# Stationary-weight products by four blocks: thirty-two high-part matmuls into four PSUM tiles, then thirty-two low-part matmuls

## The chip, the cores and the metric

One Trainium2 chip, one of its NeuronCores. A program on this core runs on TensorE (PE in the profile; PEld is its weight load), VectorE (DVE), ScalarE (ACT), GpSimd (POOL) and SyncE (SP, which issues the transfers here). The metric is the device time of one execution in microseconds (us), lower is better.

## The reference

The reference runs two transformer blocks on 256 tokens of width 1024, in fp32. The second has two layers. What matters here are its wide products, which all have the form

```python
z = rmsnorm(h) @ W            # h: 256 x 1024, W: 1024 x n
a = square(relu(u2 @ w_up))                                  # first block, n = 4096
gate, up = split(h @ w_gu); y = (silu(gate) * up) @ w_down   # four times, n = 5632
q, k, v, conv parts = split(h @ w_mix_in)                    # twice, n = 3072
k, v = split(mem @ w_kv); q = h @ w_q                        # cross attention, twice
```

The kernel keeps fp32 accuracy: each operand is split into a high part and the rest, its low part, and a product is the sum of high x high, low x high and high x low.

## The kernel before

**Weights.** `Stream` brings the weights in one fixed order (`order_of_weights`). SP loads 1 MB raw pieces (L143). `prep` makes a *unit* of two raw chunks: ScalarE copies the high part `whi` (L154), VectorE subtracts it and leaves the low part `wlo` (L155). Each kind has six buffers (`W_BUFS`), so the next `whi` or `wlo` can be written only when TensorE has read the one six units earlier. `refill` calls `prep` once for each unit that was used.

**Products.** `linear` keeps the tokens stationary and streams the weights (L364 to L366). `linear_ws` does the reverse for `w_up`, the four gate-up products (`w_ffn*_gu`, called *gu* below), `w_mix_in`, `w_xq` and the key halves of `w_xkv`: the weights are stationary. A *group* is 512 outputs, four *blocks* of 128; one unit holds the weights of one block. A block has eight matmuls over 512 columns (`highs`, L403: high weights against the high and the low part of all 256 tokens) and eight over 256 columns (`lows`, L407: low weights against the high parts). All 16 accumulate in one PSUM tile of the block. There are four such tiles (`mm_tile`, tag `mm`, four buffers), taken in turn by both `linear` and `linear_ws`. The program has 70 groups in `linear_ws`; where `halves` is set, the first group of a product (seven in all) has a path of its own, L415 to L431.

**Evacuation.** When a block is done, `evac` lets ScalarE copy the right half of the tile at once (L446, waits for the block's lows), and pushes the rest as a chain of small steps on `side`: VectorE adds the left half (L447). This *add* is the last reader of the tile; a block that takes the same buffer four blocks later waits for it with its first high matmul. Then follow, for gu, a scaling by the row of norms (L917), Silu on ScalarE (L918), the product with the gate (L925), the high copy on ScalarE (L926) and the low part (L929). `side.pump` runs one such step at each call, two when over six chains are open.

**Order.** The order that the code is written in is not the order on the engines: the framework orders each engine's instructions when the program is built, and the order is then fixed. Each engine works its queue in that order.

The added line of the evacuation, and the two steps that it comes in:

```python
def added(dst, psum):
    ACT.activation(dst, psum[:, S:], AF.Copy)
    return lambda: V.tensor_tensor(dst, psum[:, :S], dst, op=ALU.add)
```

Of the kernel before, what the change touches and what calls it, by code (L numbers as in the profile page):

```python
# [17 lines left out]
P = 128  # L18
# [158 lines left out]
def order_of_weights():  # L177
    o = []

    def full(name, gs, nch):  # L180
        for g in gs:
            for c in range(0, nch, 8):
                o.append((name, g, c, min(8, nch - c)))

    full("w_in", range(8), 8)
    full("w_branch_pool", range(2), 4)
    full("w_branch_attn", range(2), 4)
    full("w_out", range(2), 8)
    full("w_xkv_0", (0,), 8)
    full("w_up", range(8), 8)  # L190
    full("w_down", range(2), 32)
    full("w_xkv_0", (1,), 8)
    for l in range(2):
        full(f"w_ffn1_gu_{l}", range(11), 8)
        full(f"w_ffn1_down_{l}", range(2), 22)
        full(f"w_mix_in_{l}", range(6), 8)
        full(f"w_xkv_{l}", (0, 1) if l == 1 else (2,), 8)
        for c in (4, 0):
            for g in range(2):
                o.append((f"w_mix_out_{l}", g, c, 4))  # L200
        full(f"w_xq_{l}", range(2), 8)
        full(f"w_xkv_{l}", (2, 3) if l == 1 else (3,), 8)
        for c in (0, 4):
            for g in range(2):
                o.append((f"w_xo_{l}", g, c, 4))
        full(f"w_ffn2_gu_{l}", range(11), 8)
        full(f"w_ffn2_down_{l}", range(2), 22)
    return o
# [3 lines left out]
def tile_two_blocks(ctx: ExitStack, tc: tile.TileContext, A: dict, out: bass.AP):  # L212
# [11 lines left out]
    side = Side()  # L224
    W = Stream(nc, wp, order_of_weights(), A)

    def mm_tile():
        return ps.tile([P, 512], F32, name="mm", tag="mm", bufs=4)
# [165 lines left out]
    def moving(lhs, c):  # L394
        for t in range(NT):
            side.want(lhs, (t, c))
        return lhs["m", c]

    def highs(psum, w, lhs, cs, st):


        for k, c in enumerate(cs):
            PE.matmul(psum, lhsT=w[:, k], rhs=moving(lhs, c), start=st and k == 0, stop=False)  # L403

    def lows(psum, w, lhs, cs, en):
        for k, c in enumerate(cs):
            PE.matmul(psum[:, :S], lhsT=w[:, k], rhs=lhs["m", c][:, 0], start=False, stop=en and k == len(cs) - 1)  # L407

    def linear_ws(name, gs, lhs, evac, halves=False):

        for g in gs:
            key = (name, g, 0, 8)
            if halves and g == gs[0]:  # L415
                pt = [mm_tile() for b in range(4)]
                for i in range(4):
                    half, bb = i // 2, i % 2
                    hi, lo = (w.rearrange("p a (c b q) -> p (a c) b q", b=2, q=P) for w in W.get(key, i)[:2])
                    cs = range(half * 4, half * 4 + 4)  # L420
                    for b in range(2):
                        highs(pt[2 * bb + b], hi[:, :, b], lhs, cs, half == 0)
                    side.pump()
                    for b in range(2):
                        lows(pt[2 * bb + b], lo[:, :, b], lhs, cs, half == 1)
                    W.refill()
                    side.pump()
                    if half == 1:
                        for b in range(2):
                            evac(g, 2 * bb + b, pt[2 * bb + b])  # L430
                continue  # L431
            for bb in (0, 2):
                pt = [mm_tile() for b in range(2)]
                w = [[u.rearrange("p a (c q) -> p (a c) q", q=P) for u in W.get(key, bb + b)[:2]] for b in range(2)]
                for b in range(2):
                    highs(pt[b], w[b][0], lhs, range(8), True)
                    side.pump()
                for b in range(2):
                    lows(pt[b], w[b][1], lhs, range(8), True)
                    W.refill()  # L440
                    side.pump()
                    evac(g, bb + b, pt[b])

    def added(dst, psum):

# [203 lines left out]
    def mem_keys(l, gs, lhs, pool, K):  # L649

        if not K:
            row = pool.tile([P, S], F32, name="row_mem")
            K["row"] = side.push(broadcast(row, rstd_mem))
            K["r"] = row
            K["kts"] = []
        for g in gs:
            K[g] = pool.tile([P, 2, 4, S], F32R, name=f"K{g}")

        def evac(g, b, psum):
            d = held("key")[:, :S]  # L660
            add = added(d, psum)

            def high():
                add()
                V.tensor_tensor(d, d, K["r"], op=ALU.mult)
                ACT.activation(K[g][:, 0, b], d, AF.Copy)

            def low():
                V.tensor_tensor(K[g][:, 1, b], d, K[g][:, 0, b].bitcast(F32), op=ALU.subtract)
            K["kts"].append(toks.add(side.push(high, low, deps=(K["row"],))))  # L670

        linear_ws(f"w_xkv_{l}", gs, lhs, evac)
# [175 lines left out]
    with tc.tile_pool(name="h1", bufs=1) as hp:  # L848
        lhs_a = {}

        def evac_up(g, b, psum):
            X = operand(lhs_a, g, hp, f"h{g}")
            a = held("up")[:, :S]
            add = added(a, psum)

            def high():
                add()
                V.scalar_tensor_tensor(a, a, 0.0, a, op0=ALU.max, op1=ALU.mult)
                ACT.activation(X[:, b, 0], a, AF.Copy)

            def low():
                V.tensor_tensor(X[:, b, 1], a, X[:, b, 0].bitcast(F32), op=ALU.subtract)
                give(lhs_a, X, 4 * g + b, 1, b)
            side.gives(toks.add(side.push(high, low)), lhs_a, [(t, 4 * g + b) for t in range(NT)])

        linear_ws("w_up", range(8), lhs_u2, evac_up, halves=True)
        rstd_f = {}
        lhs_f, evac_dn = post_norm("norm_mlp_post", [hp.tile([P, 512], F32, name=f"y{t}") for t in range(NT)],
                                      rstd_f, "ffn1_0", hp, rstd_u2)
        linear("w_down", range(2), 32, lhs_a, evac_dn, hold=True)  # L870
# [18 lines left out]
    def swiglu(l, which, lhs, rstds, gname):  # L889
        with tc.tile_pool(name=f"h{which}_{l}", bufs=1) as hp:  # L890
# [12 lines left out]
            def evac(g, b, psum):  # L903
# [27 lines left out]
                side.gives(pairs.add(side.push(high, low, deps=(gu["c"],))), lhs_h, [(t, 2 * g + j) for t in range(NT)])  # L931

            linear_ws(f"w_ffn{which}_gu_{l}", range(11), lhs, evac, halves=True)
            rn = {}
            nlhs, ev, _ = norm_residual(gname, rn, half_r)
# [321 lines left out]
    lhs, rstds = lhs_f, rstd_f  # L1257
    for l in range(2):
        last = l == 1
        lhs, rstds = swiglu(l, 1, lhs, rstds, f"mix_{l}")  # L1260
# [5 lines left out]
        with tc.tile_pool(name=f"v{l}", bufs=1) as vp:  # L1266
            with tc.tile_pool(name=f"mix{l}", bufs=1) as mp:
                lhs, rstds = mixer(l, lhs, rstds, mp, lhs_mem, K, Vp, vp)
            with tc.tile_pool(name=f"cr{l}", bufs=1) as mp:
                lhs, rstds = cross(l, lhs, rstds, mp, lhs_mem, K, Vp)  # L1270
        kt_ctx.close()
        lhs, rstds = swiglu(l, 2, lhs, rstds, None if last else "ffn1_1")
# [109 lines left out]
```

## Time and profile before

| | |
|---|---|
| median of 3 runs | 1518.08 us (1517.91 to 1520.4) |
| the profiled execution | 1518.06 us, its span 1516.2 us |
| TensorE busy | 1504.6 us, 99% of the span, 8026 matmuls |
| VectorE busy | 1061.2 us, 70% |
| ScalarE busy | 866.3 us, 57% |
| TensorE's granted clock | 0.999 of full speed over the span |

The span is the time between the first and the last instruction of the profiled execution; 1.9 us lie around it. Matmul times in the trace overlap, since the next one starts while the last drains: how long a matmul holds TensorE is read from start to start, not from its duration.

### The profile page before, as it was taken

What the parts mean: (1) busy time and instruction counts of PE and PEld (TensorE: products, weight loads), DVE (VectorE), ACT (ScalarE), POOL (GpSimd) and SP (SyncE); (2) the same over time, 40 slices, a digit from 0 to 9 for tenths busy, and PEclk for the clock granted to TensorE, in tenths of its full rate; (3) what the DMA queues carried; (4) which work ended last, traced back from release to release, by engine and by line L of the source; (5) the groups of instructions that cost most, each with busy time, mean ns of one, the idle gap of its engine ahead of it and who ended that gap; (6) DMA issues with size and microseconds to landing.
All of it is one profiled execution on the core that took longest, in us unless ns stands there. A gap on an engine that the chain in (4) does not pass through costs nothing.

```text
span 1516.2 us, 20937 instructions
## 1 busy us (share of the span) xinstructions
PE 1504.6 (99%) x8026; PEld 1284.0 (85%) x8026; DVE 1061.2 (70%) x1690; ACT 866.3 (57%) x1463; POOL 28.3 (2%) x43
## 2 busy tenths in 40 slices
PE   9999999999999999999999999999999999999998
PEld 7888888888888888888888888888888888888886
DVE  4758887448777557887677656776578887677753
ACT  6655666346665456656565545565466656566542
POOL 0000000000000000000000000000000000000000
PEclk9999999999999999999999999999999999999999
DMA  8565555545555464454455546554564454455552
GB/s 319 188 213 200 205 195 190 183 182 195 193 182 185 163 223 142 136 195 135 152 187 193 181 167 212 191 194 153 208 223 139 151 183 152 169 175 190 191 181 70
DMA packets 43734, 276.17 MB, mean 182 GB/s; under 512 B 5489, under 2 KB 6385, under 8 KB 12145
## 3 DMA queue, kind: packets, MB, share of 16 engines
q1 hardware_dynamic: 42912, 273.78, 52.9%
q8 instruction: 63, 1.03, 0.3%
q10 hardware_dynamic: 720, 1.05, 0.2%
q14 instruction: 39, 0.31, 0.1%
HBM read 273.76 MB, written 1.05 MB: 181 GB/s over the span
## 4 chain that ended last, share of the span: by engine, by line
PE 93%; DVE 4%; issue 1%; ACT 1%; DMA 0%; POOL 0%; SPq 0%; POOLq 0%; ACTq 0%; DVEq 0%
PE mm L403 32%; PE mm L407 16%; PE mm L364 13%; PE mm L366 13%; PE mm L365 13%; DVE wlo L155 2%; PE tp L612 1%; PE tp L310 1%; PE sc L575 1%; DVE lx L327 1%; PE tp L597 1%; DVE tmpT L304 1%; DMA raw<-in_w_in 0%; PE sc L1178 0%; ACT whi L154 0%
## 5 line engine op out<-in xcount | busy, mean ns | idle before, releaser
L155 DVE TENSOR_TENSOR wlo<-raw,whi 128x1024 fp32r<-128x1024 f32 (+1 forms) x505 | 612.2, 1220 | 288.3 <-ACT whi L154 178.7
L154 ACT ACTIVATE whi<-raw 128x1024 fp32r<-128x1024 f32 (+1 forms) x505 | 532.2, 1057 | 387.1 <-PE mm L403 209.4
L403 PE MATMUL mm<-lx,whi 128*128 128x512 f32 x2240 | 545.7, 393 | 2.7 <-DVE lx L327 2.2
L403 PEld LDWEIGHTS mm<-lx,whi 128*128 128x128 f32 x2240 | 408.9, 188 | 83.7 <-DVE lx L327 3.3
L407 PEld LDWEIGHTS mm<-lx,wlo 128*128 128x128 f32 x2240 | 289.5, 191 | 12.1
L407 PE MATMUL mm<-lx,wlo 128*128 128x256 f32 x2240 | 297.7, 283 | 0.0
L364 PE MATMUL mm<-whi,h 128*128 128x512 f32 x480 | 187.4, 390 | 0.0
L365 PE MATMUL mm<-whi,h 128*128 128x512 f32 x480 | 187.1, 390 | 0.0
L366 PE MATMUL mm<-wlo,h 128*128 128x512 f32 x480 | 186.8, 389 | 0.0
L364 PE MATMUL mm<-whi,lx 128*128 128x512 f32 x288 | 114.2, 397 | 0.0
L366 PE MATMUL mm<-wlo,lx 128*128 128x512 f32 x288 | 112.6, 391 | 0.0
L365 PE MATMUL mm<-whi,lx 128*128 128x512 f32 x288 | 112.3, 390 | 0.0
L366 PEld LDWEIGHTS mm<-wlo,h 128*128 128x128 f32 x480 | 90.1, 188 | 18.8
L364 PEld LDWEIGHTS mm<-whi,h 128*128 128x128 f32 x480 | 90.1, 188 | 18.4
L365 PEld LDWEIGHTS mm<-whi,h 128*128 128x128 f32 x480 | 90.2, 188 | 18.3
L446 ACT ACTIVATE gu<-mm 128x256 f32<-128x256 f32 x176 | 65.1, 375 | 21.7 <-PE mm L407 21.7
L925 DVE TENSOR_TENSOR gu<-gu 128x256 f32<-128x256 f32 x88 | 37.4, 425 | 42.3 <-ACT gu L918 42.3
L447 DVE TENSOR_TENSOR gu<-mm,gu 128x256 f32<-128x256 f32 x176 | 66.0, 417 | 0.0
L366 PEld LDWEIGHTS mm<-wlo,lx 128*128 128x128 f32 x288 | 54.1, 188 | 11.5
L365 PEld LDWEIGHTS mm<-whi,lx 128*128 128x128 f32 x288 | 54.2, 188 | 10.2
L364 PEld LDWEIGHTS mm<-whi,lx 128*128 128x128 f32 x288 | 54.2, 188 | 10.2
L347 ACT ACTIVATE junk<-x 128x512 f32<-128x512 f32 x44 | 27.6, 626 | 58.8 <-DVE x L466 50.2
(219 smaller groups left out, 1249.8 us busy)
## 6 DMA issues: line engine op xcount, KB each, us to landing
raw<-in_w_ffn_gu SPq DMA_DIRECT2D x88, 1024.0 KB, 4.9
raw<-in_w_ffn_down SPq DMA_DIRECT2D x40, 1024.0 KB, 4.9
raw<-in_w_mix_in SPq DMA_DIRECT2D x24, 1024.0 KB, 4.9
raw<-in_w_xkv SPq DMA_DIRECT2D x16, 1024.0 KB, 4.9
raw<-in_w_up SPq DMA_DIRECT2D x16, 1024.0 KB, 4.8
raw<-in_w_down SPq DMA_DIRECT2D x16, 1024.0 KB, 4.7
raw<-in_w_in SPq DMA_DIRECT2D x14, 1024.0 KB, 5.4
raw<-in_w_mix_out SPq DMA_DIRECT2D x8, 1024.0 KB, 4.9
```

Of the source, the lines that this page charges most:

```text
L154: self.nc.scalar.activation(hi[:, :n], raw[:, j:j + n], AF.Copy)
L155: self.nc.vector.tensor_tensor(lo[:, :n], raw[:, j:j + n], hi[:, :n].bitcast(F32), op=ALU.subtract)
L304: V.tensor_tensor(tmp, psum3, g_cols.unsqueeze(2).to_broadcast([P, n, P]), op=ALU.mult)
L347: ACT.activation(junk()[:, :src.shape[-1]], src, AF.Square, scale=scale, accum_out=s)
L364: PE.matmul(psum, lhsT=xl, rhs=hi[:, j], start=st, stop=False)
L365: PE.matmul(psum, lhsT=xh, rhs=hi[:, j], start=False, stop=False)
L366: PE.matmul(psum, lhsT=xh, rhs=lo[:, j], start=False, stop=en)
L403: PE.matmul(psum, lhsT=w[:, k], rhs=moving(lhs, c), start=st and k == 0, stop=False)
L407: PE.matmul(psum[:, :S], lhsT=w[:, k], rhs=lhs["m", c][:, 0], start=False, stop=en and k == len(cs) - 1)
L446: ACT.activation(dst, psum[:, S:], AF.Copy)
L447: return lambda: V.tensor_tensor(dst, psum[:, :S], dst, op=ALU.add)
L925: V.tensor_tensor(su, su, sg, op=ALU.mult)
```

## The change

Where `linear_ws` ran a group as two pairs of blocks (sixteen highs, sixteen lows, twice), it now takes all four PSUM tiles at its start, runs the 32 highs, then the 32 lows. `side.pump` is called after each block's highs and after each block's lows, as before; `refill` and `evac` come behind each block's lows. The first groups with `halves` are not touched. 63 groups are.

```diff
-            for bb in (0, 2):
-                pt = [mm_tile() for b in range(2)]
-                w = [[u.rearrange("p a (c q) -> p (a c) q", q=P) for u in W.get(key, bb + b)[:2]] for b in range(2)]
-                for b in range(2):
-                    highs(pt[b], w[b][0], lhs, range(8), True)
-                    side.pump()
-                for b in range(2):
-                    lows(pt[b], w[b][1], lhs, range(8), True)
-                    W.refill()
-                    side.pump()
-                    evac(g, bb + b, pt[b])
+            pt = [mm_tile() for b in range(4)]
+            for b in range(4):
+                w = W.get(key, b)[0].rearrange("p a (c q) -> p (a c) q", q=P)
+                highs(pt[b], w, lhs, range(8), True)
+                side.pump()
+            for b in range(4):
+                w = W.get(key, b)[1].rearrange("p a (c q) -> p (a c) q", q=P)
+                lows(pt[b], w, lhs, range(8), True)
+                W.refill()
+                side.pump()
+                evac(g, b, pt[b])
```

The order of the built programs differs in three places that matter below.

**VectorE in a gu product.** Before, a pair of blocks (tiles `mm_4060` and `mm_4061`) stands like this; `gu_4094` holds the pair's gate and up parts, `h` the finished operand, and the `wlo` rows are the weight units made for later:

```order
L155 TENSOR_TENSOR wlo_4091<-raw_3945,whi_4090 128x1024
L929 TENSOR_TENSOR h6_3986<-gu_4040,h6_3986 128x256
L155 TENSOR_TENSOR wlo_4106<-raw_3945,whi_4105 128x1024
L447 TENSOR_TENSOR gu_4094<-mm_4060,gu_4094 128x256
L447 TENSOR_TENSOR gu_4094<-mm_4061,gu_4094 128x256
L917 TENSOR_TENSOR gu_4094<-gu_4094,row_3254 128x256
L925 TENSOR_TENSOR gu_4094<-gu_4094 128x256
```

Now a whole group of four blocks (tiles `mm_4057` to `mm_4060`), the last two rows of its fourteen left off:

```order
L155 TENSOR_TENSOR wlo_4109<-raw_3944,whi_4108 128x1024
L155 TENSOR_TENSOR wlo_4124<-raw_3944,whi_4123 128x1024
L447 TENSOR_TENSOR gu_4112<-mm_4057,gu_4112 128x256
L155 TENSOR_TENSOR wlo_4142<-raw_4018,whi_4141 128x1024
L917 TENSOR_TENSOR gu_4112<-gu_4112,row_3254 128x256
L447 TENSOR_TENSOR gu_4112<-mm_4058,gu_4112 128x256
L155 TENSOR_TENSOR wlo_4159<-raw_4018,whi_4158 128x1024
L925 TENSOR_TENSOR gu_4112<-gu_4112 128x256
L447 TENSOR_TENSOR gu_4148<-mm_4059,gu_4148 128x256
L447 TENSOR_TENSOR gu_4148<-mm_4060,gu_4148 128x256
L929 TENSOR_TENSOR h7_4113<-gu_4112,h7_4113 128x256
L917 TENSOR_TENSOR gu_4148<-gu_4148,row_3254 128x256
```

The four subtractions of a group, whose buffers come free with the group's four blocks of lows, stood two by two between pairs that lay a pair of highs apart; now they stand around the first two adds.

**TensorE in a gu product.** Before, the same pair and the start of the next:

```order
L403 MATMUL mm_4060<-lx_3140,whi_3927 128x512 x4
L403 MATMUL mm_4060<-lx_3166,whi_3927 128x512 x4
L403 MATMUL mm_4061<-lx_3140,whi_3941 128x512 x4
L403 MATMUL mm_4061<-lx_3166,whi_3941 128x512 x4
L407 MATMUL mm_4060<-lx_3140,wlo_3928 128x256 x4
L407 MATMUL mm_4060<-lx_3166,wlo_3928 128x256 x4
L407 MATMUL mm_4061<-lx_3140,wlo_3942 128x256 x4
L407 MATMUL mm_4061<-lx_3166,wlo_3942 128x256 x4
L403 MATMUL mm_4115<-lx_3140,whi_3981 128x512 x4
```

Now, from the second block of a group to the first of the next (the first block's highs and one of its lows stand just ahead):

```order
L403 MATMUL mm_4059<-lx_3168,whi_3999 128x512 x4
L403 MATMUL mm_4060<-lx_3142,whi_4014 128x512 x4
L403 MATMUL mm_4060<-lx_3168,whi_4014 128x512 x4
L407 MATMUL mm_4057<-lx_3142,wlo_3924 128x256 x3
L407 MATMUL mm_4057<-lx_3168,wlo_3924 128x256 x4
L407 MATMUL mm_4058<-lx_3142,wlo_3941 128x256 x4
L407 MATMUL mm_4058<-lx_3168,wlo_3941 128x256 x4
L407 MATMUL mm_4059<-lx_3142,wlo_4000 128x256 x4
L407 MATMUL mm_4059<-lx_3168,wlo_4000 128x256 x4
L407 MATMUL mm_4060<-lx_3142,wlo_4015 128x256 x4
L407 MATMUL mm_4060<-lx_3168,wlo_4015 128x256 x4
L403 MATMUL mm_4166<-lx_3142,whi_4032 128x512 x4
```

`mm_4166` takes the buffer of `mm_4057`: a buffer was taken again after a whole other pair had run, and now is taken right behind the group's lows, of which 31 stand in one run.

**VectorE in the mixer, where the k group of `w_mix_in` ends.** `cB` are tiles of the forget gate's bias, made from transposes (`tp`, L1024 on TensorE) that `side` puts among the lows; `kT` rows at L447 are the adds of the group's blocks (`mm_5166` is the first). Before:

```order
L155 TENSOR_TENSOR wlo_5201<-raw_5036,whi_5200 128x1024
L155 TENSOR_TENSOR wlo_5214<-raw_5036,whi_5213 128x1024
L1026 TENSOR_TENSOR cB_4932<-tp_5219,c_mask_182 128x2x128
L447 TENSOR_TENSOR kT_4925<-mm_5166,kT_4925 128x256
L447 TENSOR_TENSOR kT_4925<-mm_5167,kT_4925 128x256
L1028 TENSOR_TENSOR cB_4932<-tp_5219,c_mask_182 128x2x128
L1026 TENSOR_TENSOR cB_4932<-tp_5238,c_mask_182 128x2x128
```

Now:

```order
L155 TENSOR_TENSOR wlo_5227<-raw_5036,whi_5226 128x1024
L1028 TENSOR_TENSOR cB_4932<-tp_5210,c_mask_182 128x2x128
L1026 TENSOR_TENSOR cB_4932<-tp_5230,c_mask_182 128x2x128
L155 TENSOR_TENSOR wlo_5248<-raw_5036,whi_5247 128x1024
L1028 TENSOR_TENSOR cB_4932<-tp_5230,c_mask_182 128x2x128
L1026 TENSOR_TENSOR cB_4932<-tp_5253,c_mask_182 128x2x128
L155 TENSOR_TENSOR wlo_5271<-raw_5129,whi_5270 128x1024
L1028 TENSOR_TENSOR cB_4932<-tp_5253,c_mask_182 128x2x128
L1026 TENSOR_TENSOR cB_4932<-tp_5274,c_mask_182 128x2x128
L155 TENSOR_TENSOR wlo_5292<-raw_5129,whi_5291 128x1024
L1028 TENSOR_TENSOR cB_4932<-tp_5274,c_mask_182 128x2x128
L447 TENSOR_TENSOR kT_4925<-mm_5166,kT_4925 128x256
```

The first add stood behind two subtractions and one `cB` row, and now stands behind all four subtractions and the seven `cB` rows between them.

## Rows read from the trace of the kernel before

**Rows 1.** The page's head, and busy time by engine.
```profile
span 1516.2 us, 20937 instructions
PE 1504.6 (99%) x8026; PEld 1284.0 (85%) x8026; DVE 1061.2 (70%) x1690; ACT 866.3 (57%) x1463; POOL 28.3 (2%) x43
```

**Rows 2.** The chain that ended last, by engine, then its largest lines.
```profile
PE 93%; DVE 4%; issue 1%; ACT 1%; DMA 0%; POOL 0%; SPq 0%; POOLq 0%; ACTq 0%; DVEq 0%
PE mm L403 32%; PE mm L407 16%; PE mm L364 13%; PE mm L366 13%; PE mm L365 13%; DVE wlo L155 2%; PE tp L612 1%; PE tp L310 1%; PE sc L575 1%; DVE lx L327 1%; PE tp L597 1%; DVE tmpT L304 1%; DMA raw<-in_w_in 0%; PE sc L1178 0%; ACT whi L154 0%
```

**Rows 3.** TensorE's waits: total us, times, longest us.
```profile
PE mm L403 <- DVE lx L327: 2.2, 5, 1.6
PE mm L403 <- DVE key L447: 0.5, 2, 0.3
```

**Rows 4.** Timeline of PE in a gu product: start, us, operation, count.
```profile
449.98 3.82 PE L403 MATMUL mm<-lx,whi 128*128 128x512 f32 x16
453.63 2.08 PE L407 MATMUL mm<-lx,wlo 128*128 128x256 f32 x16
455.55 3.82 PE L403 MATMUL mm<-lx,whi 128*128 128x512 f32 x16
...
461.11 1.09 PE L403 MATMUL mm<-lx,whi 128*128 128x512 f32 x4
```

**Rows 5.** Timeline of DVE in the same pair.
```profile
454.79 1.23 DVE L155 TENSOR_TENSOR wlo<-raw,whi 128x1024 fp32r<-128x1024 f32 x1 [0.94 <-PE mm L407]
455.93 0.42 DVE L929 TENSOR_TENSOR h<-gu,h 128x256 fp32r<-128x256 f32 x1
456.26 1.22 DVE L155 TENSOR_TENSOR wlo<-raw,whi 128x1024 fp32r<-128x1024 f32 x1
457.40 0.75 DVE L447 TENSOR_TENSOR gu<-mm,gu 128x256 f32<-128x256 f32 x2
458.06 0.42 DVE L917 TENSOR_TENSOR gu<-gu,row 128x256 f32<-128x256 f32 x1
```

**Rows 6.** Timeline around 1211.7 us, where TensorE waited for an add.
```profile
1211.25 0.41 DVE L447 TENSOR_TENSOR key<-mm,key 128x256 f32<-128x256 f32 x1
...
1211.78 0.76 PEld L403 LDWEIGHTS mm<-lx,whi 128*128 128x128 f32 x4 [0.47 <-ACT whi L154]
1211.81 0.93 PE L403 MATMUL mm<-lx,whi 128*128 128x512 f32 x3 [0.29 <-DVE key L447]
```

**Rows 7.** Groups of instructions by line: x count, busy us, mean ns, idle before.
```profile
L155 DVE TENSOR_TENSOR wlo<-raw,whi 128x1024 fp32r<-128x1024 f32 (+1 forms) x505 | 612.2, 1220 | 288.3 <-ACT whi L154 178.7 <-PE mm L407 85.9 <-PE mm L365 10.3
...
L858 DVE SCALAR_TENSOR_TENSOR up<-up 128x256 f32<-128x256 f32 x32 | 12.0, 417 | 0.0
...
L580 DVE TENSOR_REDUCE nm<-S 128x4 f32<-128x512 f32 (+1 forms) x12 | 11.3, 946 | 0.0
L964 DVE SCALAR_TENSOR_TENSOR S<-sc,cq,cB 128x128 f32<-128x128 f32 (+1 forms) x32 | 11.1, 409 | 0.0
```

**Rows 8.** Timeline of the mixer's k group: DVE, then PE.
```profile
581.00 2.36 DVE L155 TENSOR_TENSOR wlo<-raw,whi 128x1024 fp32r<-128x1024 f32 x2 [0.87 <-ACT whi L154]
583.28 0.42 DVE L1026 TENSOR_TENSOR cB<-tp,c_mask 128x256 f32<-128x256 f32 x1
583.61 0.75 DVE L447 TENSOR_TENSOR kT<-mm,kT 128x256 f32<-128x256 f32 x2
...
586.25 0.60 PE L1024 MATMUL tp<-c_ident,cq 128*128 128x128 f32 x4
586.60 1.20 PE L407 MATMUL mm<-lx,wlo 128*128 128x256 f32 x8
587.64 0.60 PE L1024 MATMUL tp<-c_ident,cq 128*128 128x128 f32 x4
587.99 1.19 PE L407 MATMUL mm<-lx,wlo 128*128 128x256 f32 x8
589.02 0.86 PE L403 MATMUL mm<-lx,whi 128*128 128x512 f32 x3
```

**Rows 9.** Busy time by engine in a stretch, with granted clock before DMA share.
```profile
174.00:178.00 4.00, 2.43 (x15) 1.97 (x14) 4.00 (x9) 2.81 (x6) 0.00 (x0) 1.00 0.75 258
```

## Prediction

> **What bounds the kernel now.** The page's head says that TensorE is busy 1504.6 of 1516.2 us [rows 1], and the chain that ended last is TensorE's for 93% and VectorE's for 4% [rows 2]. The list of TensorE's waits says how little it stands: the lines of these products, L403, waited 2.2 us for `lx` and 0.5 us for a key's add [rows 3]. So a change that leaves the matmuls as they are can gain about 2.7 us, and lose whatever wait it brings. What a matmul holds is read from start to start: sixteen highs from 449.98 to 453.63 are 3.65 us, 0.228 each, and sixteen lows to 455.55 are 1.92 us, 0.12 each [rows 4]. A group takes 2 x (449.98 to 455.55) = 11.1 us.
>
> The reader should see two slacks. VectorE's rows of the same pair [rows 5] show both adds over at 457.40 + 0.75 = 458.15, and the matmul that takes the first of these buffers again starts at 461.11 [rows 4]: 3.0 us early. And VectorE is the engine on which this hangs: a low part takes 1.22 us and the next instruction starts 1.14 after it (456.26, 457.40), a small step holds it about 0.335 (454.79 + 1.14 to 456.26) and ends after 0.42. Four low parts and ten small steps for each gu group are 4 x 1.14 + 10 x 0.335 = 7.9 of 11.1 us. It has room over the group, but not at every place in it.
>
> **The change, part by part.** No instruction is added or removed. The matmuls keep shape and number, so 32 highs and 32 lows cost 11.1 us as before; a low behind a low or behind a high costs the same 0.12. What moves is when a PSUM tile is free. All four tiles belong to one group, so the next group's first high waits for the add of block 0, which can only begin when block 0's lows are done, at the end of the group. The order decides the rest: on VectorE the first add stands behind two low parts, and the four low parts stand within 31 lows instead of two and two.
>
> *gu, forty groups.* Let 0 be the start of the 31 lows. Block 0 ends its lows after 7 x 0.12 = 0.84; VectorE starts a low part 0.20 after the lows that free its buffer (454.79, against 453.63 + 8 x 0.12 = 454.59), so at 1.04. The second starts at 2.18, the add at 3.32, and the add ends at 3.32 + 0.415 = 3.74. The lows are through at 31 x 0.12 = 3.72. A late add is seen once in this trace [rows 6]: it ends at 1211.25 + 0.41 = 1211.66 and the matmul starts at 1211.81, 0.15 later, and the first three matmuls then take 0.93 us where three take 0.86 without a wait [rows 8], 0.07 more. So the high starts at 3.89 instead of 3.72, and a boundary costs 0.17 + 0.07 = 0.24 us. The next adds: add 1 stands behind a third low part and a scaling, and from the first add's start at 3.32 it ends at 3.32 + 0.335 + 1.14 + 0.335 + 0.415 = 5.55; its high, a block of highs later (3.89 + 1.82 + 0.07), is wanted at 5.78 and needs it 0.15 earlier, 5.63. That fits by 0.08. Add 2 is behind one low part and one product more, 7.36 against 7.45, and add 3 a small step later against a whole block. So only the first wait counts: 40 x 0.24 = **+9.5 us**.
>
> *w_up, seven groups.* The first add is placed as in gu, 0.24. In every second group the second add stands behind a third low part, the product at L858 (0.417 long [rows 7]), a fourth low part and another small step: it ends 4 x 1.14 + 3 x 0.335 + 0.42 = 5.98 after the first low part's start, at 7.02. TensorE runs the first highs and, there, eight lows before the second highs, wanting them at 3.89 + 0.07 + 1.82 + 0.96 = 6.74: 0.43 late with the 0.15, and 0.07 for the restart. Boundaries then cost 0.24 + 0.5 and, in the other groups, about 0.2; three pairs and a last one are **+3 us**.
>
> *Mixer, two layers, five groups each.* Behind the k group the lows stand among four sets of transposes. Before, a set took from 586.25 to 586.60, and the eight lows behind it 1.04 instead of 0.96 [rows 8]: 0.44 in all. Run: 31 x 0.12 + 4 x 0.44 = 5.5 us. VectorE's first low part starts at 0.44 + 0.84 + 0.20 = 1.5; then four low parts and seven `cB` rows stand ahead of the add: 1.5 + 4 x 1.14 + 7 x 0.335 + 0.42 = 8.8, where before two low parts and one `cB` row stood ahead (581.00 to 583.61 [rows 8]). The high starts at 8.95 instead of 5.5 and costs 0.07: 3.5 us, and I take 3.6, since the sets use two buffers that VectorE also frees late: **+7.2** for two layers. Behind the zc group the late one is the second add. It stands behind three low parts, a row maximum L580 (mean 0.95, at least 0.6), three small steps and four S rows L964 (0.41 long, about 0.3 each on) [rows 7]: 3.42 + 0.6 + 1.0 + 1.2 + 0.42 = 6.6 from a start at 1.04, so 7.7, against about 6.2 where TensorE, with scores and transposes between its blocks, wants it: 1.6, **+3.2**. Behind zb the first add has three low parts ahead of it and ends at 1.04 + 3.42 + 0.42 = 4.88 against 3.84; 0.15 and 0.07 make 1.4, less two sets of transposes (0.8) that stand first: 0.6, **+1.2**. Behind q, with its transposes of `cums`, and behind uT, with eight and more small matmuls among the lows, nothing is late.
>
> *Keys of the second layer.* Their first adds too have three low parts ahead, and the second add a fourth and two small steps: about 1.8 between the two groups and 1.4 to what follows, less the 0.5 us that stood there before [rows 3]: **+2.7**.
>
> *Keys of the first layer.* Here the change removes a wait, the longest in the kernel, 1.6 us for `lx` [rows 3]. The chain of `lx` now has a group's 7.3 us of highs to finish in. But the later `lx` of the same token tile then comes about 0.7 us late, and the adds of the key groups cost some tenths: **-0.4**.
>
> The queue of SP is not touched by this: a group uses the same raw pieces in the same 11 us; the high parts on ScalarE move into the highs, where it has 57% to do [rows 1]. I cost that at nothing; were ScalarE late by a high part (1.06 us) once in a product, it would be under 8 us in all, and the range holds that.
>
> Sum: 9.5 + 3.0 + 7.2 + 3.2 + 1.2 + 2.7 - 0.4 = 26.4 us. The profiled execution took 1518.06 us, 1.9 more than its span, and the median is 1518.08, so the forecast stands on either: **1544.5 us**.
>
> **A rule to weigh.** The 1.6 us that TensorE waited left no mark on its clock: from 174 to 178 us, with the wait in it, the granted clock is 1.00 [rows 9], the 2.4 GHz level. The Trainium skill, in "TensorE: Matmul & The Clock Gate", section "A second HAM failure mode: psum-queue depth-cycling", describes a kernel that cycles through PSUM banks, whose TensorE idles a little between groups of matmuls so often that its clock swings between its two levels. By the trace the clock adds nothing to the sum; by that rule it is rival 4.
>
> **The rivals.** 1. *The tile is free in time (no slower, or a little faster).* The gu add is late by 0.02 us against the end of the lows; a weight load comes 0.03 ahead of its matmul at a restart and 0.12 after the add [rows 6]. If VectorE reached the add about 0.28 us earlier (one low part of 0.86 instead of 1.14 would do, or an order that lets the add go first), all forty waits would vanish; were the mixer's hidden as well, what is left is the `lx` wait that goes: 1518 - 1.6 = 1516.5, or no change if the keys eat it. Against it: the order has the two low parts ahead of the add, and 505 low parts have a mean of 1220 ns [rows 7], with no sign of a faster one. 7 in 100, 3 of them faster by over 0.2%. That bound, 3 us, is about what a measurement of this kernel can tell from no change.
>
> 2. *Less is lost.* If a boundary's restart costs only 0.1 and the mixer's TensorE work, as it slips, gives VectorE half its lateness back, gu is 4, w_up 2, mixer and keys 7: 13 us, 1531. For it: waits in a chain overlap, and one late add makes the next fit. 20 in 100.
>
> 3. *More is lost.* If every mixer boundary is as late as zc's or k's (10 more) and VectorE's rest of a group reaches into the next group's w_up and key adds (5 more), the time is 1560. For it: VectorE has 70% to do in the mean [rows 1], and what it falls behind in the mixer it carries on. 15 in 100.
>
> 4. *The clock falls.* If each of some 57 waits set the next block of highs (1.82 us) to the lower level of 1.2 GHz, it would take 1.82 us more: 57 x 1.82 = 104, and 1648 us. Against it: rows 9. 2 in 100. That is the case the page's rule would make.
>
> **How the numbers follow.** The forecast itself (1536 to 1553) has 56 in 100, rival 2 twenty, rival 3 fifteen, rival 1 seven, the clock two. The range from 1529 to 1561 takes in the forecast and most of rivals 2 and 3, and leaves out the first and the last and the far ends, some 15 in 100. Slower by over 0.2% is everything but rival 1: 93 in 100; the same 4; faster 3.
>
> **What would show it.** The list of TensorE's waits should have a new first row, L403 for gu's L447, with forty waits of 0.1 to 0.2 us, then rows for `kT` and `zc` (longest about 3.5) and for the second layer's keys; the `lx` wait should shrink. VectorE's busy time should stay at 1061 us, the clock at 1.00, and the highs and lows at 0.228 and 0.12. Wrong would be: VectorE's first add starting ahead of a low part, waits on `whi` or `wlo` (then weights, not PSUM, are late), or gu boundaries with no gap.

## The result, and the profile after

The changed kernel takes 1544.22 us in the median of four executions (1544.1 to 1547.25) against 1518.2, a ratio of 1.0174 (95% interval 1.0162 to 1.0187): slower by 26.0 us. The forecast was 1544.5. The profiled execution is the longest of the four, 1547.25 us; why it is 3 us over the others is part of the answer below.

The head of its page, with busy time by engine, answers to [rows 1]:

```profile
span 1545.3 us, 21062 instructions
PE 1520.9 (98%) x8026; PEld 1290.5 (84%) x8026; DVE 1056.4 (68%) x1690; ACT 881.3 (57%) x1463; POOL 27.1 (2%) x43
```

The work is the same: 8026 matmuls, 1690 VectorE instructions. VectorE is no busier (1056 us, 1061 before). The span grew by 29.1 us, so TensorE stood or ran slower. TensorE's waits (total us, times, longest) answer to [rows 3]:

```profile
PE mm L403 <- DVE kT L447: 6.2, 2, 3.1
PE mm L502 <- DVE junk L499: 1.5, 1, 1.5
PE sc L575 <- DVE S L964: 1.3, 2, 0.7
PE mm L403 <- DVE lx L327: 1.2, 4, 0.7
PE mm L364 <- DVE key L447: 1.0, 1, 1.0
PE mm L403 <- DVE up L447: 0.9, 3, 0.3
PE tp L1012 <- DVE lf L1008: 0.9, 2, 0.5
PE mm L364 <- ACT whi L154: 0.7, 2, 0.5
PE mm L403 <- ACT whi L154: 0.7, 1, 0.7
PE tp L612 <- DVE PT L599: 0.5, 2, 0.3
```

The 1.6 us wait for `lx` is gone (0.7 is the longest left), and the adds at L447 have come in its place. The list has no row for gu, though forty boundaries were to wait there. In the rows below, the record of the last low still runs (422.15 + 3.87 = 426.02) when the next high starts at 425.93, so the profile sees TensorE busy through the gap; only starts show it. TensorE's timeline through two gu groups, beside [rows 4]:

```profile
414.59 2.11 PE L403 MATMUL mm<-lx,whi 128*128 128x512 f32 x8
...
422.15 3.87 PE L407 MATMUL mm<-lx,wlo 128*128 128x256 f32 x31
425.93 2.11 PE L403 MATMUL mm<-lx,whi 128*128 128x512 f32 x8
...
433.46 3.87 PE L407 MATMUL mm<-lx,wlo 128*128 128x256 f32 x31
437.25 0.97 PE L403 MATMUL mm<-lx,whi 128*128 128x512 f32 x3
```

From 414.59 to 425.93 is 11.34 us, to 437.25 another 11.32, where a group took 11.13. The VectorE rows of the same place, beside [rows 5], show the two low parts and then the add, over at 425.46 + 0.42 = 425.88, the high at 425.93:

```profile
423.18 2.36 DVE L155 TENSOR_TENSOR wlo<-raw,whi 128x1024 fp32r<-128x1024 f32 x2 [1.73 <-PE mm L407]
425.46 0.42 DVE L447 TENSOR_TENSOR gu<-mm,gu 128x256 f32<-128x256 f32 x1
```

Behind the k group of the mixer the wait is plain, in the timeline of VectorE and TensorE that answers to [rows 8]:

```profile
596.31 1.21 DVE L155 TENSOR_TENSOR wlo<-raw,whi 128x1024 fp32r<-128x1024 f32 x1
...
597.44 0.42 DVE L1028 TENSOR_TENSOR cB<-tp,c_mask 128x256 f32<-128x256 f32 x1
597.77 0.74 DVE L447 TENSOR_TENSOR kT<-mm,kT 128x256 f32<-128x256 f32 x2
598.24 1.69 PEld L403 LDWEIGHTS mm<-lx,whi 128*128 128x128 f32 x7 [3.29 <-DVE kT L447]
598.24 1.98 PE L403 MATMUL mm<-lx,whi 128*128 128x512 f32 x6 [3.09 <-DVE kT L447]
```

And here the prediction's sum has no term for what follows. The windows behind this wait (after the engines' busy times, the granted clock stands ahead of the DMA share):

```profile
594.00:598.00 4.00, 1.15 (x10) 0.95 (x9) 4.00 (x8) 1.33 (x4) 0.00 (x0) 1.00 0.73 254
...
600.00:602.00 2.00, 2.00 (x6) 1.59 (x5) 0.94 (x3) 0.89 (x1) 0.00 (x0) 0.50 0.86 365
602.00:604.00 2.00, 2.00 (x8) 1.59 (x8) 0.00 (x0) 0.33 (x2) 0.00 (x0) 0.79 0.00 0
604.00:608.00 4.00, 4.00 (x24) 2.94 (x22) 1.64 (x5) 1.96 (x2) 0.00 (x0) 1.00 0.00 0
```

Soon after TensorE comes back, the granted clock is 0.50, the 1.2 GHz level, in which six highs fill 2 us instead of nine, and then 1.00 again. In the second layer, behind an equal wait, it stays at the lower level longer (13 slow highs instead of 7):

```profile
1170.00:1176.00 6.00, 5.71 (x13) 4.46 (x14) 3.00 (x9) 1.06 (x1) 0.00 (x0) 0.50 0.55 191
```

The table sets each stretch of the program against the kernel before, in us. A stretch runs from the first high of its first group to the first high of what follows it, as the two traces give them (the last one to the last matmul). Small matmuls that moved across a border count where they ran, so neighbouring rows are read together. e1 to e4 are the first four experiments, below.

| stretch | before | after | e1 adds first | e2 gu only | e3 mixer only | e4 k in pairs |
|---|---|---|---|---|---|---|
| keys 0, first layer | 14.93 | -1.31 | +0.40 | 0.00 | 0.00 | -1.31 |
| w_up and w_down | 176.29 | +3.45 | -0.17 | 0.00 | 0.00 | +3.39 |
| keys 1, first layer | 12.95 | +0.24 | +2.01 | -0.01 | -0.01 | +0.24 |
| gu, four products | 760.89 | +7.82 | -1.46 | +7.12 | +0.07 | +7.36 |
| q and k, layer 1 | 27.27 | +4.12 | +0.19 | 0.00 | +4.08 | +0.72 |
| zc, layer 1 | 14.47 | +1.73 | +0.87 | 0.00 | +0.06 | -0.04 |
| uT and zb, layer 1 | 66.89 | +1.57 | +0.08 | 0.00 | +1.61 | +1.61 |
| q and k, layer 2 | 27.27 | +4.18 | +0.30 | 0.00 | +4.14 | +0.77 |
| zc, layer 2 | 14.46 | +2.86 | +0.87 | 0.00 | +0.06 | -0.04 |
| uT and zb, layer 2 | 31.49 | +2.41 | +0.10 | +0.01 | +2.43 | +2.41 |
| keys, layer 2 | 47.37 | +1.74 | -0.39 | 0.00 | -0.40 | +1.79 |

### The profile page after: what moved, and what is told of

Its sections match the earlier page's. It is cut to its first block, busy times and chain, and to the rows that moved or that the text cites. A ratio compares the mean times of both kernels' runs of the same rounds, so it can differ in the third digit from the quotient of the medians.

```text
span 1545.3 us, 21062 instructions
## 1 busy us (share of the span) xinstructions
PE 1520.9 (98%) x8026; PEld 1290.5 (84%) x8026; DVE 1056.4 (68%) x1690; ACT 881.3 (57%) x1463; POOL 27.1 (2%) x43
## 4 chain that ended last, share of the span: by engine, by line
PE 88%; DVE 7%; ACT 2%; issue 1%; DMA 1%; POOL 0%; SPq 0%; POOLq 0%; DVEq 0%; ACTq 0%
PE mm L403 32%; PE mm L407 14%; PE mm L364 13%; PE mm L366 13%; PE mm L365 13%; DVE wlo L155 3%; PE tp L612 1%; ACT whi L154 1%; PE tp L310 1%; DMA raw<-in_w_in 0%; DVE lx L327 0%; DVE tmpT L304 0%; PE tp L597 0%; DVE S L964 0%; ACT junk L347 0%
## 5 line engine op out<-in xcount | busy, mean ns | idle before, releaser
L154 ACT ACTIVATE whi<-raw 128x1024 fp32r<-128x1024 f32 (+1 forms) x505 | 531.6, 1056 | 292.9 <-PE mm L365 148.8
L407 PEld LDWEIGHTS mm<-lx,wlo 128*128 128x128 f32 x2240 | 285.3, 191 | 10.0 <-issue 0.7
L364 PE MATMUL mm<-whi,h 128*128 128x512 f32 x480 | 188.0, 392 | 0.0
L364 PE MATMUL mm<-whi,lx 128*128 128x512 f32 x288 | 113.9, 396 | 1.2 <-DVE key L447 1.0
L364 PEld LDWEIGHTS mm<-whi,h 128*128 128x128 f32 x480 | 90.1, 188 | 19.0
L447 DVE TENSOR_TENSOR gu<-mm,gu 128x256 f32<-128x256 f32 x176 | 69.5, 416 | 0.5 <-ACT gu L446 0.5
L364 PEld LDWEIGHTS mm<-whi,lx 128*128 128x128 f32 x288 | 54.2, 188 | 11.8 <-DVE key L447 1.3
```

Of the source, the lines that this page charges most:

```text
L154: self.nc.scalar.activation(hi[:, :n], raw[:, j:j + n], AF.Copy)
L364: PE.matmul(psum, lhsT=xl, rhs=hi[:, j], start=st, stop=False)
```

## The experiments

The theory: what is lost is the wait for VectorE's add, the last reader of a PSUM tile, since the low parts of the coming weights stand ahead of it in VectorE's queue. The rivals: the order of the matmuls itself costs (through PSUM, or weights that come late); or VectorE's load, not its order.

**e1, the adds first.** In the changed kernel:

```diff
     def added(dst, psum):
         ACT.activation(dst, psum[:, S:], AF.Copy)
-        return lambda: V.tensor_tensor(dst, psum[:, :S], dst, op=ALU.add)
+        V.tensor_tensor(dst, psum[:, :S], dst, op=ALU.add)
+        return lambda: None
...
                 lows(pt[b], w, lhs, range(8), True)
+                evac(g, b, pt[b])
                 W.refill()
                 side.pump()
-                evac(g, b, pt[b])
```

> Four blocks as in the changed kernel, but each add is written in the evacuation itself, and the evacuation ahead of the refill, so that on VectorE an add stands behind at most one low part of its group instead of two to four. If the late adds are the cause, the 40 gu boundaries lose nothing (0.18 to 0.21 us each now), the 3.1 us waits behind the two k groups go, the clock stays at 1.00 there, and the time is 1516 to 1520 us. If the four-block order itself costs (weights that come late, or TensorE going through four PSUM tiles), the gaps stay and the time is 1538 to 1545 us. If the mixer's lateness is VectorE's load and not its order, gu is free and the mixer still waits: about 1530 us.

Measured: 1522.28 us (1521.25 to 1523.03), ratio to the kernel before 1.0025 (1.0015 to 1.0036). TensorE still runs 32 highs and then 32 lows, and 22 of the 26 us are gone. In a gu group VectorE now has the first add behind one low part, and TensorE's rows show 11.11 us from group to group (401.73 to 412.84):

```profile
401.73 7.44 PE L403 MATMUL mm<-lx,whi 128*128 128x512 f32 x32
409.01 4.00 PE L407 MATMUL mm<-lx,wlo 128*128 128x256 f32 x32
412.84 3.36 PE L403 MATMUL mm<-lx,whi 128*128 128x512 f32 x14
```

The waits for `kT` are out of the list and the clock is 1.00 behind the k groups. The expectation of 1516 to 1520 missed by 2 us. The list of the profiled execution, the shortest of the eight, says where: adds that go first push back another VectorE step, the low part of `lx`, which cost 2.2 us before [rows 3]:

```profile
PE mm L403 <- DVE lx L327: 4.1, 4, 2.1
```

**e2, gu alone**, and **e3, the mixer alone**. The pairs of the kernel before stand beside the four blocks under one condition, here that of e2; in e3 it is `'mix_in' in name`:

```diff
+            if '_gu_' in name:
+                pt = [mm_tile() for b in range(4)]
...
+            else:
+                for bb in (0, 2):
+                    pt = [mm_tile() for b in range(2)]
```

> Four blocks in the gu products alone, pairs everywhere else. Late adds: 40 boundaries of 0.18 to 0.2 us and nothing else, +7.5 us on the kernel before, about 1525.7 us, clock 1.00 throughout. If the gaps depended on what the other products leave behind, it would be under 1521 us.

Measured: 1525.46 us (1524.9 to 1525.74), ratio 1.0045 (1.0029 to 1.0062), clock 0.999. The forty boundaries are worth 7.2 us, and in the table nothing else moves.

> Four blocks in w_mix_in alone, pairs everywhere else. Each theory expects the 3.1 us wait behind the k group, twice. If the clock falls because of that one wait, the granted clock is 0.5 for a few us behind it here too, with no gu gaps in the program, and the time is 15 to 17 us over the kernel before, 1533 to 1535 us. If the clock falls because of the many small gaps before it, it stays at 1.00 here and the time is 10 to 12 us over, 1528 to 1530 us.

Measured: 1532.84 us (1530.12 to 1533.47), ratio 1.0092 (1.0077 to 1.0107). The profiled execution is the shortest, and has the full wait and no fall. TensorE's rows and then the windows behind the first k group:

```profile
593.18 5.73 PE L403 MATMUL mm<-lx,whi 128*128 128x512 f32 x24 [3.09 <-DVE kT L460]
```
```profile
593.00:595.00 2.00, 1.82 (x8) 1.52 (x9) 2.00 (x7) 0.00 (x0) 0.00 (x0) 1.00 0.79 184
595.00:597.00 2.00, 2.00 (x11) 1.65 (x10) 0.89 (x3) 1.06 (x1) 0.00 (x0) 1.00 0.90 377
```

The 24 highs take 5.73 us, where the same stretch of the changed kernel took 7.39. The waits are the same; whether the clock falls behind one is not. The other three executions are 2.1 to 3.4 us longer than this one, about what one or two falls cost, though without their traces that is inferred. So neither expectation held as written. The small gaps are not what it takes: e7, below, has none in gu, and the clock fell behind one of its two k groups.

**e4, the k groups in pairs.** The condition is `if not ('mix_in' in name and g == 2)`.

> The changed kernel with the two k groups of w_mix_in back in pairs. If the first add behind four low parts and seven rows of the forget gate's bias is what waits, both 3.1 us waits go and with them the fall of the clock (about 1.9 us behind the first wait, 3.0 behind the second): 10 us less than the changed kernel, about 1534 us; if the zc group's adds then wait as the prediction counted (1.6 us a layer), about 1537 us. If the wait is due to VectorE's load in the mixer, it moves to the next boundary, and the time is over 1541 us.

Measured: 1535.22 us, ratio 1.0111 (1.0096 to 1.0126), 9.0 under the changed kernel. `kT` is out of the list of waits, nothing has come in its place behind k or zc, the clock is 1.00 behind both, and the four executions lie within 0.4 us (1535.14 to 1535.46), where the changed kernel's lie within 3.2. That fits a scatter that comes from these waits, but does not show it: e1, which has none of them, lies within 1.8 us, and of the first four executions of the kernel before one took 1520.4.

**e5 and e6, the add made later.** A step more ahead of the first add of each gu group, into a tile that nothing reads: of 256 columns in e5, and in e6 of 1792, with both inputs broadcast seven times:

```diff
                     def gate():
+                        if b == 0 and g > 0:
+                            V.tensor_tensor(late, sg, row, op=ALU.mult)
                         add()
```

> The changed kernel with one small VectorE step more (the gate by the row, into a tile that nothing reads) ahead of the first add of each of the 40 gu groups; in the built order the add then stands behind a third low part and this step, 1.14 + 0.335 = 1.475 us more of VectorE. If TensorE waits for that add, each boundary grows by 1.475 us, 59 us in all, about 1602 us, with forty waits of about 1.5 us for gu's add in the list. If the gap of 0.18 to 0.2 us is a fixed cost of coming back to the first PSUM tile, it is under 1550 us. If waits of this length already lower the clock, as the fourth rival has it, the granted clock shows 0.5 behind the boundaries and the time is 1640 to 1680 us.

Measured: 1605.93 us (1604.45 to 1607.41), ratio 1.0576 (1.056 to 1.0593), 3.9 over what was expected of a wait for the add. TensorE's rows: 12.84 us from group to group, 1.5 more than in the changed kernel for 1.475 us more of VectorE.

```profile
406.07 7.54 PE L403 MATMUL mm<-lx,whi 128*128 128x512 f32 x32 [1.48 <-DVE gu L447]
...
418.91 7.52 PE L403 MATMUL mm<-lx,whi 128*128 128x512 f32 x32 [1.47 <-DVE gu L447]
```

By as much as VectorE's add is later, TensorE stands. The list has 36 such waits ahead of a high, and four of 1.4 to 1.5 us where a product ends. No fall of the clock follows any of them; over nine groups the window has

```profile
390.00:496.00 106.00, 92.73 (x528) 80.89 (x528) 71.22 (x126) 57.15 (x99) 0.00 (x0) 1.00 0.49 161
```

> As the run with one more small step, but that step is 128 x 1792, about 2.0 us, so that the add is late by 1.14 + 2.0 = 3.15 us at each of the 40 boundaries, as long as the wait behind the k group. Without any fall of the clock: 40 x 3.15 = 126 us more than the changed kernel, about 1669 us. If each wait of this length makes the clock fall, 1.7 to 2.9 us more at each, 1735 to 1785 us, with 0.5 behind every boundary. If it falls behind some waits and not behind others, as between the two executions of the mixer-only kernel, the time lies between and the profile shows both kinds.

Measured: 1742.19 us (1735.93 to 1747.14), ratio 1.1472 (1.1448 to 1.1497). The waits are 3.07 us, as meant, and groups with and without a fall stand side by side:

```profile
441.12 9.16 PE L403 MATMUL mm<-lx,whi 128*128 128x512 f32 x32 [3.07 <-DVE gu L447]
450.12 3.99 PE L407 MATMUL mm<-lx,wlo 128*128 128x256 f32 x32
457.18 7.52 PE L403 MATMUL mm<-lx,whi 128*128 128x512 f32 x32 [3.07 <-DVE gu L447]
...
487.65 10.18 PE L403 MATMUL mm<-lx,whi 128*128 128x512 f32 x32 [3.07 <-DVE gu L447]
```
```profile
441.00:446.00 5.00, 4.88 (x14) 3.87 (x15) 3.63 (x9) 2.09 (x4) 0.00 (x0) 0.66 0.61 198
...
457.00:462.00 5.00, 4.82 (x21) 4.04 (x22) 3.93 (x10) 2.98 (x5) 0.00 (x0) 1.00 0.57 188
...
486.60:487.60 1.00, 0.00 (x0) 0.00 (x0) 1.00 (x3) 0.00 (x0) 0.00 (x0) 0.50 1.01 418
```

Counted over the trace, by highs that start 0.4 to 0.6 us apart: the clock fell behind 28 of the 36 gu waits, for 6 to 8 highs (1.3 to 1.6 us lost; here 9.16 - 7.52 = 1.64) or for 13 (10.18 - 7.52 = 2.66). It fell behind the four waits at the ends of the products too. The profile shows both kinds, the third case of the expectation, though with so many falls the time lies in the range of the second.

**e7, gu's tile to ScalarE.** VectorE's order is left as in the changed kernel, and ScalarE alone frees the tile:

```diff
+    def copied(dst, psum):
+        ACT.activation(dst, psum, AF.Copy)
+        return lambda: V.tensor_tensor(dst[:, :S], dst[:, :S], dst[:, S:], op=ALU.add)
...
-                    gu["s"] = hp.tile([P, 2, S], F32, name="gu", tag="gu", bufs=3)
+                    gu["s"] = hp.tile([P, 2, 2 * S], F32, name="gu", tag="gu", bufs=3)
...
-                    add = added(sg, psum)
+                    add = copied(gu["s"][:, 0], psum)
...
```

> The changed kernel with VectorE's order as it is, but in gu ScalarE copies the whole tile to SBUF (512 instead of 256 columns, about 0.25 us more each) and VectorE adds the two halves there, so that PSUM is free without VectorE. If the gap is the wait for VectorE's release, the 40 gaps go: 7.5 us less, about 1536.7 us. If VectorE's order starves something else (low parts or operands), they stay and the time is 1543 to 1546 us. If the longer copies make ScalarE late with the high parts, it is slower than the changed kernel.

Measured: 1536.53 us (1536.14 to 1537.61), ratio 1.0121 (1.0107 to 1.0135), 7.7 under the changed kernel. VectorE's add still stands behind two low parts and ends at 424.89 + 0.42 = 425.31; TensorE has gone on at 425.30 without it, because ScalarE had the tile out at 422.63 + 0.58 = 423.21:

```profile
422.62 2.36 DVE L155 TENSOR_TENSOR wlo<-raw,whi 128x1024 fp32r<-128x1024 f32 x2 [1.85 <-PE mm L407]
422.63 0.58 ACT L445 ACTIVATE gu<-mm 128x512 f32<-128x512 f32 x1
...
424.89 0.42 DVE L446 TENSOR_TENSOR gu<-gu 128x256 f32<-128x256 f32 x1
...
425.30 6.08 PE L403 MATMUL mm<-lx,whi 128*128 128x512 f32 x26
```

That rules out the matmul order, PSUM itself and starved weights as the cause of the gu gaps. One detail of TensorE's order differs: the changed kernel runs one low of a gu group's first block among the highs, while e1, e5, e6 and e7 run all 32 lows together. The waits of e5 and e6 stand without that low, so it is not the cause either.

**e8, the parts that pay.** Four blocks in gu, with the adds first as in e1, and in the first layer's first key group; pairs elsewhere. `now` writes the copy and the add at once.

```diff
+            if '_gu_' in name or (name == 'w_xkv_0' and gs[0] == 0):
...
+                    if '_gu_' in name:
+                        evac(g, b, pt[b])
                     W.refill()
                     side.pump()
+                    if '_gu_' not in name:
+                        evac(g, b, pt[b])
...
-                    add = added(sg, psum)
+                    add = now(sg, psum)
...
```

> Four blocks only where the runs show a gain: the gu products, with each add written in the evacuation and ahead of the refill (0.19 us less a product than before), and the first key group of the first layer (1.3 us less there, 0.9 given back in the group behind it). Pairs everywhere else. About 1.2 us faster than the kernel before, 1517.0 us. If the adds that go first make the operand of the next product late, as in the run with the adds first, no gain or up to 2 us slower.

Measured: 1517.36 us (1516.77 to 1517.86, eleven executions) against 1518.31 (1517.83 to 1518.79), ratio 0.9994 (0.9985 to 1.0002). The medians lie 0.95 us apart, as forecast to 0.3 us, but the interval reaches over 1, so it is not shown to be faster. In its trace the key group gives 1.31 and w_up takes 0.89 back, as in the changed kernel, and the gu products give 0.8 together.

## Why the prediction was right, point by point

**The cause holds; that the sum came so close is in part luck.** The forecast sum was +26.4 us, the median came out at +26.0, but with an estimated 1.4 us of slow clock in it (below) that the forecast did not count, and with terms that missed both ways. The main step, that the first add ends just behind the run of lows because two low parts stand ahead of it, is shown from three sides: moving the add (e1), freeing the tile without it (e7), and delaying it (e5).

**The terms were less exact than the sum.** *gu*: predicted 0.24 a boundary and 9.5 in all, measured 7.2 (e2): 0.17 to 0.21 at most boundaries and 0.05 at the first of each product. The term that was mis-sized is the start behind the add: the high came 0.05 us behind the add's end (425.88, 425.93), not 0.15 as read from [rows 6], so the gap between lows and highs was 0.07 and not 0.17. The first high then held TensorE 0.10 longer than usual (0.33, not 0.23), near the 0.07 of the sum. *w_up*: 3.0 predicted. Seven boundaries gave 0.05 to 0.67 each, 2.55 together, alternating as the order said. *Behind k*: 3.6 predicted a layer, 3.1 of wait measured, which is 3.3 lost from the start of the last low to that of the high (3.45 us, where 0.12 is usual); with 0.4 to 0.5 where the transposes of `cums` wait for `lf`, which the prediction had put at nothing, q and k lose 4.1 together. *Behind zc*: the wait for zc's second add, 1.6, is not there (e4: -0.04, with nothing slowing the highs). VectorE's lateness shows one stretch on, where the scores wait 0.7 us for S and a transpose 0.3 for PT, 1.2 in all. The prediction had the lateness of VectorE right and the instruction that feels it wrong. *zb*: 0.6 predicted (by its own terms, 4.88 - 3.84 + 0.15 + 0.07 - 0.8, it is 0.5), 0.4 measured in the first layer and 1.2 in the second. But 0.8 of that 1.2 are eight transposes (L310) that ran among the matmuls of the next stretch before. First the rows of the kernel before, then those of the changed one:

```profile
1199.61 1.03 PE L310 MATMUL tp<-c_ident,att 128*128 128x128 f32 x8
1200.40 2.16 PE L407 MATMUL mm<-lx,wlo 128*128 128x256 f32 x16
```
```profile
1220.32 1.04 PE L310 MATMUL tp<-c_ident,att 128*128 128x128 f32 x8
1221.52 2.14 PE L403 MATMUL mm<-lx,whi 128*128 128x512 f32 x8 [0.17 <-DVE zb L447]
```

So zb is 0.4 late there too. *Keys*: second layer 2.7 predicted; the table has 1.7, and with the 0.8 that moved out of this stretch 2.5 are lost. In the first layer -0.4 was predicted; the first key group gave 1.3, w_up's first group took 0.9 back and the second key group 0.2, so -0.2. Over the mixer alone the errors cancel: 5.8 a layer predicted, in e3's shortest execution 5.75 and 6.6, with the 0.8 of the transposes in the second.

**The signs.** VectorE's first add did stand behind its low parts and the `lx` wait shrank. Three signs that the prediction named came out otherwise: the list has no row for gu and none for `zc`, and the clock did not stay at 1.00. Of its signs of being wrong one shows in part: TensorE waits 0.7 us for a high part, `whi`, once in the second layer's keys, and twice ahead of L364 (0.7 in all), where the kernel before has no such row. ScalarE's lateness, which was costed at nothing, is under 1.5 us in all.

**What the sum lacked was the clock.** The two falls behind the k groups cost about 1.7 us (1.73 against 0.06 in e3) and 2.8 us in the profiled execution. Its median companions are 3 us shorter, which fits one long fall fewer. Without any, the changed kernel would stand near 1547.25 - 4.5 = 1542.8, as an estimate; so the waits alone come to some 24.6 us, and smaller terms made room for an effect that the sum had at nothing. The fourth rival, a fall behind each of 57 waits, did not come; behind two of them it did. What misled was [rows 9]: it shows that a wait of 1.6 us leaves the clock alone, which e5 confirms 36 times, and it was used for a wait of 3.5 us, for which no row stood. The Trainium skill, in "TensorE: Matmul & The Clock Gate", section "A second HAM failure mode: psum-queue depth-cycling", says of one kernel that short idling between its groups of matmuls makes the clock swing between its levels. In the traces here the clock fell behind most waits of 3.0 to 3.1 us and behind no shorter one; the longest of those is 2.1 us, e1's wait for `lx`.

**The rivals.** The one on the other side, the tile free in time, needed the gu add 0.28 us earlier; it was not, and e1 shows what an order gives in which the add goes first. "More is lost" and "less is lost" both rested on VectorE's load in the mixer; e4 shows that k's wait goes with k's order alone and is not passed on.

## What to carry to other kernels

When a loop takes all the PSUM tiles at once, ask which instruction releases the first one and what stands ahead of it in that engine's queue: here two subtractions that nobody was waiting for held back an add that TensorE was waiting for, while VectorE was busy for 68% of the span. The profile's list of waits shows none of the forty short gaps, so compare the period of a loop from start to start. And price a long wait with what may follow it: a row on a short wait says nothing about a longer one.

## What was not expected of the hardware

Behind a wait of 3.07 to 3.09 us of TensorE the granted clock fell to 0.50 in some cases and not in others: 28 of 36 in e6's gu groups, and behind the k groups twice in the changed kernel, in e5 and in e6, once in e7 and not at all in e3's profiled execution, 7 of 10. Behind 36 waits of 1.47 to 1.48 us it never fell. A fall lasted for 6 to 8 highs or for 13, and cost 1.3 to 1.7 or 2.6 to 2.8 us. In e6's gu groups all falls of 13 highs had begun before TensorE came back (as at 486.60:487.60 above), and most of the short ones began after. What decides whether and when the clock falls stays open.
